# One more pair of k tiles in seven products per weight block, and two low parts of each block made by an adding DMA

## The chip, the core and the metric

One core of one Trainium2 chip runs the kernel. The metric is the device time of one execution in microseconds (us). The engines are named as in the profile: PE is TensorE (PEld its weight loads), DVE is VectorE, ACT is ScalarE, POOL is GpSimd, and SP is SyncE, which only issues transfers here. A part of the change that moves the time by less than 0.2% (2.9 us) is called no change.

## The reference, cut to what matters

A decoder layer on 256 tokens of width 2048, in float32. One projection feeds a retention branch and a windowed attention branch; both are gated, merged and projected, and a gated feed-forward network follows:

```
proj = h @ w_in                     # retention q, k, v, g; attention q, k, v; two gates
ret = retention_branch(...) ; att = sliding_window_sink_attention(...)
merged = sigmoid(gate_a) * ret + sigmoid(gate_b) * att
h = layer_norm(alpha * h + merged @ w_out)
ffn = (silu(h @ w_gate) * (h @ w_up)) @ w_down      # 5632 wide between
h = layer_norm(alpha * h + ffn)
```

Nearly all the work is in the products with the weights: h is 256 x 2048, and w_in, w_out, w_gate, w_up and w_down are read once each.

## The kernel before, in words

**Products in three passes.** Every weight block of 128 x 2048 numbers is loaded as `raw` (1 MB), rounded by ACT to `wh`, and DVE subtracts: `wl = raw - wh`. PE then adds three products, with the high part of the activations times `wh`, the high part times `wl`, and the low part times `wh`. One such product is one matmul of 128 x 128 by 128 x 512.

**Pairs in seven products.** The retention values with their gates (7 pairs of 512-column blocks, `w_ip`, called the retention pairs here) and ten of the eleven gate/up pairs (`w_gu`) are computed two column blocks at a time by `PairChunk`. Such a chunk walks over 8 pairs of k tiles. A plain pair (`s`) has 2 x 2 x 2 block products, 8 in all, so 24 matmuls. A pair taken by a scheme of seven products (`R` with 3, then `T` with 4) has 21 matmuls, but needs sums of its weight tiles: DVE makes `tsum` from `raw` in three instructions (L290 to L292), ACT rounds it to `th` (L304), DVE makes `tl` (L305); `R` takes `wh` and `wl` of three of the tiles. Sums of the activations are made once by `hsums`. `pair_seq` writes the order: `R T s R T s ...`, and the plain pairs that are left over at the end. Before, a gate/up chunk has 3 such pairs (NQ = 3) and 5 plain ones, a retention chunk 2 (NX = 2) and 6.

**Buffers.** There are 3 buffers for `wh`/`wl` (pool `spl`), shared by `R` and `s`, one for `th`/`tl` (`sp2`), one `tsum`, and 3 for `raw`. SP issues a load of `raw` as soon as the buffer's last reader is done.

**Leaving PSUM.** A chunk adds into all 8 banks: four intermediate sums and four output tiles. When the last `T` is done, `mids` copies one sum (ACT) and adds the others up (4 DVE instructions, L735 to L738); when the chunk is done, `done_gu` adds the four output tiles (L962 to L969), with a Silu of ACT between. The result `sg2` has one buffer. It is transposed by PE (L540, 8 small matmuls, two banks) in the next chunk, by a background job that `flush` starts in `mids` and `pump` advances after each step. In the retention chunks `head`, `inner` and `gate_bg` do the corresponding work.

**What sets the order.** `Stream.ahead` issues loads and casts as far ahead as the buffers allow; a scheduler then writes each engine's queue, which the engine runs in order. The gate/up pairs come in three parts, with chunks 1 to 3, 4 to 7 and 8 to 10 (chunk 0 is not a pair), and after each part four output blocks of `w_down`, whose products are plain.

Of the kernel before, what the change touches and what calls it, by code (L numbers as in the profile page):

```python
# [9 lines left out]
F32 = mybir.dt.float32  # L10
# [6 lines left out]
P = 128  # L17
# [82 lines left out]
def layer_kernel(ctx, tc, a, out):  # L100
# [58 lines left out]
    class Chunk:  # L159
        def __init__(self, src, nk, lhs, done, sizes=None, order=None, wide=False):  # L160
            self.wide = wide
            self.src, self.nk, self.lhs, self.done = src, nk, lhs, done
            sizes = sizes or [KB] * (nk // KB)
            self.blocks = []
            self.steps = []
            k = 0
            for n in sizes:
                self.blocks.append((k, n))
                for i in range(0, n, KS):
                    m = min(KS, n - i)  # L170
# [76 lines left out]
    class PairChunk:  # L247
        FORM = {"R": (("P1", "A11", 0), ("C11", "A12", 1), ("C12", "S4", 2)),
                "T": (("P5", "S1", 0), ("P7", "S3", 1), ("P6", "S2", 2), ("C21", "A22", 3))}
        def __init__(self, src, seq, lhs, lhs_s, mid, done, quiet=False):  # L250
# [34 lines left out]
        def cast(self, i):  # L285
            u, kp, b = self.steps[i]
            r = self.raw[b]
            if u == "R":
                x = sc["tp"].tile([P, 4, C], F32, name="tsum")
                nc.vector.tensor_sub(out=x[:, 0:2], in0=r[:, 0:1].broadcast_to([P, 2, C]), in1=r[:, 1:4:2])  # L290
                nc.vector.tensor_sub(out=x[:, 2], in0=r[:, 1], in1=x[:, 1])
                nc.vector.tensor_sub(out=x[:, 3], in0=r[:, 2], in1=x[:, 2])  # L292
                self.tsum = x
            if u == "T":
                h = sc["sp2"].tile([P, KS, C], F32R, name="th")
                l = sc["sp2"].tile([P, KS, C], F32R, name="tl")
# [42 lines left out]
    class Stream:  # L339
# [323 lines left out]
    sl = {}  # L663

    def head(j):
        v = gp.tile([P, 2, C], F32, name="v")
        gg = gp.tile([P, C], F32, name="gg")
        gb = gp.tile([P, C], F32, name="gb")
        nc.sync.dma_start(out=gg, in_=bcast_cols(a["gn_g"], j * C, C))
        nc.sync.dma_start(out=gb, in_=bcast_cols(a["gn_b"], j * C, C))  # L670
        y = gp.tile([P, 2, C], F32, name="y")
        sl[j] = (y, v, gg, gb)

    def done_rv(ch, t, j):
        if t == 0:
            head(j)
        y, v, gg, gb = sl[j]
        nc.scalar.copy(out=v[:, t], in_=ch.acc[t])
        if t:
            jobs["y", j] = Job(inner(j, v, y, gg, gb), [jobs["sc", j // 2]])  # L680

    def inner(j, v, y, gg, gb):
        for t in range(2):
            ps = bank("mx", [P, C])
            nc.tensor.matmul(ps, lhsT=st_all[:, j, t * P:(t + 1) * P], rhs=v[:, 0], start=True, stop=t == 0)  # L685
            if t:
                nc.tensor.matmul(ps, lhsT=st_all[:, j, 256:384], rhs=v[:, 1], start=False, stop=True)
# [53 lines left out]
    def done_va(ch, j):  # L741
# [215 lines left out]
    def done_gu(ch, f):  # L957
# [89 lines left out]
    sc["sh"] = hp.tile([P, 4, NQ, P], F32R, name="sh")  # L1047
    sc["sl"] = hp.tile([P, 4, NQ, P], F32R, name="sl")
# [104 lines left out]
```

## Time and profile before

| | |
|---|---|
| median of 3 runs | 1440.97 us (1440.94 to 1441.03) |
| the profiled execution | 1440.99 us, span 1439.2 us, so 1.8 us lie around the span |
| PE busy | 1432.2 us of the span |
| DVE busy | 1047.2 us |
| ACT busy | 673.9 us |
| POOL busy | 0.9 us |
| matmul instructions in the program | 6338 before, 6287 after |

Read it by what ends last: the share of an engine over the whole span is an average over stages with different limits, and a stage is bound by the engine on which the others wait in that stage.

### The profile page before, as it was taken

The page shows a single profiled execution, that of the slowest core. Times are in us where ns is not written, and L with a number is a line of the kernel's source. Part 1 is how long each engine was busy: PE and PEld are TensorE (multiplying, and loading weights), DVE is VectorE, ACT ScalarE, POOL GpSimd, SP SyncE. Part 2 cuts the span into 40 slices and gives each one's busy share as a digit, 9 for nine tenths or more (in the row PEclk, how much of TensorE's full clock was granted, in tenths as well). Part 3 has the DMA queues.
Part 4 walks back from the last instruction along what each step waited for, and adds up shares of the span by engine and source line. Part 5 has one row for each costly group of instructions (what it writes and reads, how often), then busy time and mean ns, then how long its engine had stood idle before and what let it go on. Part 6 is the DMA issues. An engine that isn't in the chain of part 4 may idle for free.

```text
span 1439.2 us, 16027 instructions
## 1 busy us (share of the span) xinstructions
PE 1432.2 (100%) x6536; PEld 1174.7 (82%) x6536; DVE 1047.2 (73%) x1127; ACT 673.9 (47%) x637; POOL 0.9 (0%) x6
## 2 busy tenths in 40 slices
PE   9999999999999999999999999999999999999998
PEld 7878888878878878788888888888888888888886
DVE  6764555487879879766688996567898755799756
ACT  5465444344545445444355454344555434454432
POOL 0000000000000000000000000000000000000000
PEclk9999999999999999999999999999999999999999
DMA  8643433455555655577445645555655555555562
GB/s 325 226 152 117 147 117 118 146 178 209 198 204 179 216 189 200 182 282 262 161 144 205 228 181 193 188 196 191 227 180 208 194 178 204 205 198 207 195 223 83
DMA packets 40233, 274.73 MB, mean 191 GB/s; under 512 B 4704, under 2 KB 4832, under 8 KB 8160
## 3 DMA queue, kind: packets, MB, share of 16 engines
q1 hardware_dynamic: 39440, 272.79, 53.3%
q8 instruction: 51, 0.84, 0.2%
q10 hardware_dynamic: 720, 0.92, 0.2%
q14 instruction: 22, 0.18, 0.0%
HBM read 271.60 MB, written 2.10 MB: 190 GB/s over the span
## 4 chain that ended last, share of the span: by engine, by line
PE 98%; DVE 1%; DMA 0%; ACT 0%; SPq 0%; issue 0%
PE bank L324 16%; PE bank L326 16%; PE bank L325 16%; PE acc L235 9%; PE acc L233 9%; PE acc L234 9%; PE bank L234 6%; PE bank L235 6%; PE bank L233 6%; PE tr L540 2%; PE mx L589 1%; PE mx L618 1%; PE bank L540 1%; DMA xraw<-in_xw 0%; PE bank L685 0%; PE mx L656 0%
## 5 line engine op out<-in xcount | busy, mean ns | idle before, releaser
L218 DVE TENSOR_TENSOR wl<-raw,wh 128x2048 fp32r<-128x2048 f32 x108 | 247.1, 2290 | 171.8 <-ACT wh L217 171.5
L304 ACT CAST wh<-raw 128x2048 fp32r<-128x2048 f32 (+1 forms) x136 | 241.2, 1773 | 229.2 <-PE bank L326 161.6
L217 ACT CAST wh<-raw 128x2048 fp32r<-128x2048 f32 x108 | 206.2, 1910 | 301.7 <-PE acc L235 108.5
L305 DVE TENSOR_TENSOR wl<-raw,wh 128x2048 fp32r<-128x2048 f32 (+1 forms) x136 | 287.0, 2115 | 61.7 <-ACT wh L304 61.2
L324 PE MATMUL bank<-wh,hh 128*128 128x512 f32 x460 | 179.6, 391 | 0.0
L326 PE MATMUL bank<-wh,hl 128*128 128x512 f32 x460 | 179.1, 389 | 0.0
L325 PE MATMUL bank<-wl,hh 128*128 128x512 f32 x460 | 179.0, 389 | 0.0
L324 PE MATMUL bank<-wh,xh 128*128 128x512 f32 x364 | 144.5, 397 | 0.0
L326 PE MATMUL bank<-wh,xl 128*128 128x512 f32 x364 | 141.8, 389 | 0.0
L325 PE MATMUL bank<-wl,xh 128*128 128x512 f32 x364 | 141.7, 389 | 0.0
L233 PE MATMUL acc<-wh,xh 128*128 128x512 f32 x352 | 141.0, 402 | 0.0
L235 PE MATMUL acc<-wh,xl 128*128 128x512 f32 x352 | 138.7, 394 | 0.0
L234 PE MATMUL acc<-wl,xh 128*128 128x512 f32 x352 | 137.9, 392 | 0.5 <-DVE wl L218 0.5
L233 PE MATMUL bank<-wh,ph 128*128 128x512 f32 x352 | 137.2, 390 | 0.0
L235 PE MATMUL bank<-wh,pl 128*128 128x512 f32 x352 | 137.0, 389 | 0.0
L234 PE MATMUL bank<-wl,ph 128*128 128x512 f32 x352 | 136.9, 389 | 0.0
L305 DVE TENSOR_TENSOR tl<-tsum,th 128x2048 fp32r<-128x2048 f32 x44 | 100.8, 2290 | 21.4 <-ACT th L304 21.1
L304 ACT CAST th<-tsum 128x2048 fp32r<-128x2048 f32 x44 | 84.2, 1914 | 63.1 <-DVE tsum L292 42.9
L326 PEld LDWEIGHTS bank<-wh,hl 128*128 128x128 f32 x460 | 86.4, 188 | 18.0
L324 PEld LDWEIGHTS bank<-wh,hh 128*128 128x128 f32 x460 | 86.4, 188 | 17.8
L325 PEld LDWEIGHTS bank<-wl,hh 128*128 128x128 f32 x460 | 86.4, 188 | 17.7
L324 PEld LDWEIGHTS bank<-wh,xh 128*128 128x128 f32 x364 | 68.3, 188 | 15.8 <-issue 1.4
(250 smaller groups left out, 2100.2 us busy)
## 6 DMA issues: line engine op xcount, KB each, us to landing
raw<-in_w_gu SPq DMA_DIRECT2D x88, 1024.0 KB, 4.9
raw<-in_w_ip SPq DMA_DIRECT2D x56, 1024.0 KB, 4.9
raw<-in_w_down SPq DMA_DIRECT2D x44, 1024.0 KB, 4.9
raw<-in_w_in SPq DMA_DIRECT2D x40, 1024.0 KB, 4.9
raw<-in_w_out SPq DMA_DIRECT2D x16, 1024.0 KB, 5.2
xraw<-in_xw SPq DMA_DIRECT2D x7, 768.0 KB, 6.7
hres<-in_x SPq DMA_DIRECT2D x1, 2048.0 KB, 7.5
out_h<-hres SPq DMA_DIRECT2D x5, 256.0 KB, 2.4
```

What stands on the lines that cost most here:

```text
L217: nc.scalar.copy(out=h[:, 0:m], in_=r)
L218: nc.vector.tensor_sub(out=l[:, 0:m], in0=r, in1=h[:, 0:m].bitcast(F32))
L233: nc.tensor.matmul(self.acc[t], lhsT=xh, rhs=wh[:, j], start=st, stop=False)
L234: nc.tensor.matmul(self.acc[t], lhsT=xh, rhs=wl[:, j], start=False, stop=False)
L235: nc.tensor.matmul(self.acc[t], lhsT=xl, rhs=wh[:, j], start=False, stop=sp)
L304: nc.scalar.copy(out=h_, in_=r)
L305: nc.vector.tensor_sub(out=l_, in0=r, in1=h_.bitcast(F32))
L324: nc.tensor.matmul(self.acc[p], lhsT=xh, rhs=wh[:, j], start=st, stop=False)
L325: nc.tensor.matmul(self.acc[p], lhsT=xh, rhs=wl[:, j], start=False, stop=False)
L326: nc.tensor.matmul(self.acc[p], lhsT=xl, rhs=wh[:, j], start=False, stop=sp)
L540: m = nc.tensor.transpose(ps[:, i], s, ident)
L589: nc.tensor.matmul(sps[u][:, i], lhsT=qT[u * HD:(u + 1) * HD, h // 2], rhs=kT[u * HD:(u + 1) * HD, g, 0:W], start=True, stop=True)
```

## The change

NQ goes from 3 to 4 and NX from 2 to 3: each gate/up chunk has 4 pairs in seven products and 4 plain ones, `R T s` four times over; each retention chunk has 3 and 5. In each chunk two of the plain pairs are `far`: gate/up the second and the fourth, and the retention chunks likewise two. Of a far pair DVE makes no `wl`. ACT writes `-wh` into the buffer of `wl`, and a DMA issued by POOL reads the weight block from memory a second time and adds it in place. Its load and its casts are moved ahead of the `R` and `T` of the pair of tiles before it (`corder`). The retention values `v` move into the buffers `sg`, a `drain()` is added at the end of each part, and the activation sums of the feed-forward part get a pool of their own.

```
@@ -28,8 +28,8 @@
 NWARM = 3
 TD = 14
 CP = 1
-NQ = 3
-NX = 2
+NQ = 4
+NX = 3
 PG = 4
 NGEN = 3
 PC = 2
@@ -171,6 +171,7 @@
                     self.steps.append((k + i, m, len(self.blocks) - 1, i))
                 k += n
             ns = len(self.steps)
+            self.corder = range(ns)
             self.order = order(ns) if order else [(i, (0, 1)) for i in range(ns)]
             self.raw = {}
             self.hl = {}
@@ -247,7 +248,7 @@
     class PairChunk:
         FORM = {"R": (("P1", "A11", 0), ("C11", "A12", 1), ("C12", "S4", 2)),
                 "T": (("P5", "S1", 0), ("P7", "S3", 1), ("P6", "S2", 2), ("C21", "A22", 3))}
-        def __init__(self, src, seq, lhs, lhs_s, mid, done, quiet=False):
+        def __init__(self, src, seq, lhs, lhs_s, mid, done, quiet=False, far=()):
             self.quiet = quiet
             self.src, self.blocks, self.lhs, self.lhs_s, self.mid, self.done = src, seq, lhs, lhs_s, mid, done
             self.steps = []
@@ -302,7 +310,11 @@
                 if u == "R":
                     r, h_, l_ = r[:, 1:4], h[:, 0:3], l[:, 0:3]
             nc.scalar.copy(out=h_, in_=r)
-            nc.vector.tensor_sub(out=l_, in0=r, in1=h_.bitcast(F32))
+            if i in self.far:
+                nc.scalar.activation(out=l_, in_=h_.bitcast(F32), func=AF.Copy, scale=-1.0)
+                nc.gpsimd.dma_start(out=l_, in_=self.src[kp], accum_op=ALU.add)
+            else:
+                nc.vector.tensor_sub(out=l_, in0=r, in1=h_.bitcast(F32))
             self.hl[i] = (h, l)
 
         def mm(self, i, ts):
@@ -346,9 +358,13 @@
             self.precast = {}
 
         def add(self, ch):
-            nb = len(self.blocks)
-            self.blocks += [(ch, b) for b in range(len(ch.blocks))]
-            self.casts += [(ch, i, nb + st[2]) for i, st in enumerate(ch.steps)]
+            at = {}
+            for i in ch.corder:
+                b = ch.steps[i][2]
+                if b not in at:
+                    at[b] = len(self.blocks)
+                    self.blocks.append((ch, b))
+                self.casts.append((ch, i, at[b]))
             self.steps += [(ch, i, ts) for i, ts in ch.order]
 
         def ahead(self):
@@ -663,7 +679,7 @@
     sl = {}
 
     def head(j):
-        v = gp.tile([P, 2, C], F32, name="v")
+        v = [gp.tile([P, C], F32, name="sg", bufs=4) for _ in range(2)]
         gg = gp.tile([P, C], F32, name="gg")
         gb = gp.tile([P, C], F32, name="gb")
         nc.sync.dma_start(out=gg, in_=bcast_cols(a["gn_g"], j * C, C))
@@ -800,7 +816,7 @@
     for i in range(7):
         j = (i + 1) // 2
         stream.add(PairChunk([a["w_ip"][i, kp] for kp in range(KT // 2)], pair_seq(NX), lhs_x, lhs_xs, mids,
-                             lambda ch, j=j, f=done_va if i % 2 else done_rb: f(ch, j), quiet=True))
+                             lambda ch, j=j, f=done_va if i % 2 else done_rb: f(ch, j), quiet=True, far=(NX + 1, NX + 3)))
     mark_p = len(stream.steps)
     mark_b = mark_p + 3
 
@@ -969,6 +985,7 @@
         nc.vector.tensor_mul(out=sg[:, 1], in0=sg[:, 1], in1=x5)
         ev["u"] = [(sg, t, *pTs[f]) for t in range(2)]
         if f + 1 in (4, 8, 11):
+            drain()
             flush()
 
     parts = ((0, 4), (4, 8), (8, 11))
@@ -983,7 +1000,7 @@
                 mark_u = len(stream.steps)
             else:
                 stream.add(PairChunk([a["w_gu"][f - 1, kp] for kp in range(KT // 2)], seq, lhs_h, lhs_s, mid_gu,
-                                     lambda ch, f=f: done_gu(ch, f)))
+                                     lambda ch, f=f: done_gu(ch, f), far=(NQ + 1, NQ + 3)))
         if part == 2:
             mark_e = len(stream.steps)
         nk = (f1 - f0) * 4
@@ -1056,6 +1071,9 @@
     gsc.close()
     msc.close()
 
+    hq = fsc.enter_context(tc.tile_pool(name="hq", bufs=1))
+    sc["sh"] = hq.tile([P, 4, NQ, P], F32R, name="sh")
+    sc["sl"] = hq.tile([P, 4, NQ, P], F32R, name="sl")
     ppc = ctx.enter_context(ExitStack())
     sc["pp"] = ppc.enter_context(tc.tile_pool(name="pp", bufs=4, side=RIGHT))
     sc["tp"] = ppc.enter_context(tc.tile_pool(name="tp", bufs=1, side=RIGHT))
```

How this moves instructions shows on three queues. Line numbers of the changed kernel are larger: L298 to L300 are the sums, L312 the casts, L314 the negation, L315 the adding DMA, L317 the low parts. First DVE, in the middle of the third gate/up chunk, before:

```order
L305 TENSOR_TENSOR wl_6176<-raw_6031,wh_6175 128x1536
L305 TENSOR_TENSOR wl_6214<-raw_6104,wh_6213 128x2048 [waits DMAHW3_49,Activation_49]
L305 TENSOR_TENSOR tl_6208<-tsum_6171,th_6207 128x2048 [waits Activation_49]
L290 TENSOR_TENSOR tsum_6244<-raw_6134 128x1024 [waits DMAHW4_49,DVE_49]
L291 TENSOR_TENSOR tsum_6244<-raw_6134,tsum_6244 128x512 [waits DVE_49]
L292 TENSOR_TENSOR tsum_6244<-raw_6134,tsum_6244 128x512 [waits DVE_49]
L305 TENSOR_TENSOR wl_6249<-raw_6134,wh_6248 128x1536 [waits Activation_49]
L305 TENSOR_TENSOR wl_6280<-raw_6211,wh_6279 128x2048 [waits DMAHW5_49,Activation_49]
L305 TENSOR_TENSOR tl_6274<-tsum_6244,th_6273 128x2048 [waits Activation_49]
```

and now, at the same place:

```order
L317 TENSOR_TENSOR wl_6283<-raw_6202,wh_6282 128x1536 [waits Activation_49]
L299 TENSOR_TENSOR tsum_6278<-raw_6202,tsum_6278 128x512 [waits DVE_49]
L300 TENSOR_TENSOR tsum_6278<-raw_6202,tsum_6278 128x512 [waits DVE_49]
L317 TENSOR_TENSOR tl_6303<-tsum_6278,th_6302 128x2048 [waits Activation_49]
L317 TENSOR_TENSOR wl_6338<-raw_6208,wh_6337 128x1536 [waits DMAHW4_49,Activation_49]
L298 TENSOR_TENSOR tsum_6333<-raw_6208 128x1024 [waits DVE_49]
L317 TENSOR_TENSOR wl_6369<-raw_6264,wh_6368 128x2048 [waits DMAHW5_49,Activation_49]
L299 TENSOR_TENSOR tsum_6333<-raw_6208,tsum_6333 128x512 [waits DVE_49]
L300 TENSOR_TENSOR tsum_6333<-raw_6208,tsum_6333 128x512 [waits DVE_49]
L317 TENSOR_TENSOR tl_6363<-tsum_6333,th_6362 128x2048 [waits Activation_49]
```

Before, the low parts of `R` and of a plain pair stand between the last sum and `tl`; now `tl` stands right behind the sum from which ACT must first make `th`. So it is for three of the four sums in six of the ten gate/up chunks and for one sum in another; for one of three in six retention chunks.

Second ACT, at the hand-over from the second to the third gate/up chunk, before (the two Silu are ACTIVATE of `sg2`):

```order
L304 CAST wh_6096<-raw_5986 128x1536 [waits DMAHW0_49]
L304 CAST wh_6130<-raw_6016 128x2048 [waits DMAHW1_49,PE_49,Activation_49]
L963 ACTIVATE sg2_6160<-sg2_6160 128x512 [waits DVE_49]
L304 CAST wh_6175<-raw_6031 128x1536 [waits DMAHW2_49,PE_49,Activation_49]
L966 ACTIVATE sg2_6160<-sg2_6160 128x512 [waits DVE_49]
L304 CAST wh_6213<-raw_6104 128x2048 [waits DMAHW3_49,PE_49,Activation_49]
```

and now:

```order
L312 CAST th_6198<-tsum_6160 128x2048 [waits DVE_49,PE_49,Activation_49]
L312 CAST wh_6259<-raw_6134 128x2048 [waits DMAHW2_49,PE_49]
L417 CAST ph_5945<-bank_6245 128x4x128 [waits PE_49]
L417 CAST ph_5945<-bank_6250 128x4x128 [waits PE_49]
L314 ACTIVATE wl_6260<-wh_6259 128x2048 [waits DMASW1_49,Activation_49]
L979 ACTIVATE sg2_6234<-sg2_6234 128x512 [waits DVE_49]
L982 ACTIVATE sg2_6234<-sg2_6234 128x512 [waits DVE_49]
```

The eviction of the transposed tiles and the negation for the next chunk's first far pair now stand ahead of the two Silu.

Third PE, at the same hand-over. Before, the last plain pair is followed by the next chunk's `R` (`bank` numbers are new tiles in the 8 banks):

```order
L325 MATMUL bank_5925<-wl_6028,hh_4762 128x512
L326 MATMUL bank_5925<-wh_6027,hl_4763 128x512
L324 MATMUL bank_6179<-wh_6096,hh_4762 128x512 [waits DVE_49,Activation_49]
L325 MATMUL bank_6179<-wl_6097,hh_4762 128x512 [waits DVE_49]
L326 MATMUL bank_6179<-wh_6096,hl_4763 128x512
L324 MATMUL bank_6183<-wh_6096,hh_4762 128x512
L325 MATMUL bank_6183<-wl_6097,hh_4762 128x512
L326 MATMUL bank_6183<-wh_6096,hl_4763 128x512
L324 MATMUL bank_6187<-wh_6096,sh_4764 128x512 [waits PE_49]
L325 MATMUL bank_6187<-wl_6097,sh_4764 128x512
```

and now:

```order
L338 MATMUL bank_6007<-wh_6094,hl_4825 128x512
L556 MATMUL bank_6245<-cst_80,sg2_5944 128x128 [waits Activation_49]
L556 MATMUL bank_6245<-cst_80,sg2_5944 128x128 x3
L556 MATMUL bank_6250<-cst_80,sg2_5944 128x128 [waits DVE_49]
L556 MATMUL bank_6250<-cst_80,sg2_5944 128x128 x3
L336 MATMUL bank_6266<-wh_6164,hh_4824 128x512 [waits DVE_49]
L337 MATMUL bank_6266<-wl_6165,hh_4824 128x512
L338 MATMUL bank_6266<-wh_6164,hl_4825 128x512
L336 MATMUL bank_6270<-wh_6164,hh_4824 128x512 [waits DVE_49]
L337 MATMUL bank_6270<-wl_6165,hh_4824 128x512
L338 MATMUL bank_6270<-wh_6164,hl_4825 128x512
L336 MATMUL bank_6274<-wh_6164,sh_5469 128x512 [waits DVE_49]
```

The transposes of the first chunk's result now stand at this hand-over, where before they stood two plain pairs (48 matmuls) ahead of it, and the first three products of `R` each wait for DVE to empty a bank. At the first hand-over of each of the three parts there are no transposes.

## Rows read from the trace of the kernel before

**Rows 1.** The page: busy time of the engines, and the chain by engine.

```profile
PE 1432.2 (100%) x6536; PEld 1174.7 (82%) x6536; DVE 1047.2 (73%) x1127; ACT 673.9 (47%) x637; POOL 0.9 (0%) x6
...
PE 98%; DVE 1%; DMA 0%; ACT 0%; SPq 0%; issue 0%
```

**Rows 2.** Windows: two gate/up chunks; two retention pairs. Columns in the first row.

```profile
core 0: us, PE busy (x) PEld busy (x) DVE busy (x) ACT busy (x) POOL busy (x), PEclk, DMA share, GB/s
1001.00:1042.50 41.50, 41.50 (x185) 34.36 (x184) 36.70 (x30) 21.01 (x15) 0.00 (x0) 1.00 0.57 203
1042.50:1084.70 42.20, 42.20 (x192) 35.02 (x191) 37.91 (x32) 21.75 (x17) 0.00 (x0) 1.00 0.56 199
385.67:473.56 87.89, 87.89 (x388) 71.79 (x387) 74.39 (x72) 44.05 (x34) 0.00 (x0) 1.00 0.55 196
```

**Rows 3.** Timeline of PE, 27 matmuls apart; the last `T` of that next chunk.

```profile
984.69 0.39 PE L324 MATMUL bank<-wh,hh 128*128 128x512 f32 x1
...
990.81 0.39 PE L324 MATMUL bank<-wh,hh 128*128 128x512 f32 x1
...
1043.85 0.39 PE L324 MATMUL bank<-th,sh 128*128 128x512 f32 x1
```

**Rows 4.** The chain in order of time: transposes of one gate/up result.

```profile
1052.18 0.87 PE bank L540 x8
```

**Rows 5.** Timeline of DVE in gate/up chunks: start, duration, idle before and releaser.

```profile
994.32 2.29 DVE L305 TENSOR_TENSOR wl<-raw,wh 128x2048 fp32r<-128x2048 f32 x1 [0.71 <-ACT wh L304]
...
1001.80 1.23 DVE L290 TENSOR_TENSOR tsum<-raw 128x1024 f32<-128x1024 f32 x1 [2.15 <-DMA raw<-in_w_gu]
...
1011.89 2.29 DVE L305 TENSOR_TENSOR tl<-tsum,th 128x2048 fp32r<-128x2048 f32 x1 [0.74 <-ACT th L304]
1014.10 1.75 DVE L305 TENSOR_TENSOR wl<-raw,wh 128x1536 fp32r<-128x1536 f32 x1
...
1021.15 0.68 DVE L964 TENSOR_TENSOR w<-w,bank 128x512 f32<-128x512 f32 x1
1021.75 0.68 DVE L965 TENSOR_TENSOR sg<-vx,bank 128x512 f32<-128x512 f32 x1
...
1030.64 1.22 DVE L290 TENSOR_TENSOR tsum<-raw 128x1024 f32<-128x1024 f32 x1
...
1033.37 1.76 DVE L305 TENSOR_TENSOR wl<-raw,wh 128x1536 fp32r<-128x1536 f32 x1
...
1038.56 2.29 DVE L305 TENSOR_TENSOR tl<-tsum,th 128x2048 fp32r<-128x2048 f32 x1 [0.47 <-ACT th L304]
...
1055.41 1.28 DVE L402 TENSOR_TENSOR pl<-bank,ph 128x512 fp32r<-128x512 f32 x2
```

**Rows 6.** Timeline of DVE in a retention pair, one sum and its `tl`.

```profile
441.07 0.68 DVE L292 TENSOR_TENSOR tsum<-raw,tsum 128x512 f32<-128x512 f32 x1
443.73 2.29 DVE L305 TENSOR_TENSOR tl<-tsum,th 128x2048 fp32r<-128x2048 f32 x1 [1.98 <-ACT th L304]
```

**Rows 7.** Groups by line and form: count, busy us, mean ns, idle before.

```profile
L305 DVE TENSOR_TENSOR wl<-raw,wh 128x2048 fp32r<-128x2048 f32 x92 | 210.0, 2288 | 54.3 <-ACT wh L304 54.1
...
L304 ACT CAST wh<-raw 128x2048 fp32r<-128x2048 f32 x92 | 176.0, 1913 | 156.8 <-PE bank L326 111.6 <-issue 36.9 <-PE bank L235 7.9
...
L304 ACT CAST wh<-raw 128x1536 fp32r<-128x1536 f32 x44 | 65.2, 1482 | 72.4 <-PE bank L326 50.0 <-issue 11.9 <-DVE hres L881 7.0
```

**Rows 8.** DMA issues: count, size, median us from issue to landing.

```profile
raw<-in_w_gu SPq DMA_DIRECT2D x88, 1024.0 KB, 4.9
raw<-in_w_ip SPq DMA_DIRECT2D x56, 1024.0 KB, 4.9
```

**Rows 9.** Waits of SP's queue: us in total, times, longest.

```profile
SPq L282 <- DVE wl L305: 569.7, 119, 9.2
```

More of the change, by code (lines that the diff above doesn't have):

```diff
@@ L30 @@
 CP = 1
-NQ = 3
-NX = 2
+NQ = 4
+NX = 3
 PG = 4
@@ L173, in __init__ @@
             ns = len(self.steps)
+            self.corder = range(ns)
             self.order = order(ns) if order else [(i, (0, 1)) for i in range(ns)]
@@ L249, in layer_kernel, with __init__ @@
                 "T": (("P5", "S1", 0), ("P7", "S3", 1), ("P6", "S2", 2), ("C21", "A22", 3))}
-        def __init__(self, src, seq, lhs, lhs_s, mid, done, quiet=False):
+        def __init__(self, src, seq, lhs, lhs_s, mid, done, quiet=False, far=()):
             self.quiet = quiet
@@ L266, in __init__ @@
             self.last_s = max([i for i, st in enumerate(self.steps) if st[0] == "T"], default=-1)
+            self.far = {i for i, st in enumerate(self.steps) if st[0] == "s" and st[1] in far}
+            self.corder = []
+            for i, (u, kp, b) in enumerate(self.steps):
+                at = len(self.corder)
+                if i in self.far:
+                    at -= 2 if self.steps[i - 1][0] == "T" else 1
+                self.corder.insert(at, i)
         def parts(self, u, kp):
@@ L304, in cast @@
             nc.scalar.copy(out=h_, in_=r)
-            nc.vector.tensor_sub(out=l_, in0=r, in1=h_.bitcast(F32))
+            if i in self.far:
+                nc.scalar.activation(out=l_, in_=h_.bitcast(F32), func=AF.Copy, scale=-1.0)
+                nc.gpsimd.dma_start(out=l_, in_=self.src[kp], accum_op=ALU.add)
+            else:
+                nc.vector.tensor_sub(out=l_, in0=r, in1=h_.bitcast(F32))
             self.hl[i] = (h, l)
@@ L348, in add @@
         def add(self, ch):
-            nb = len(self.blocks)
-            self.blocks += [(ch, b) for b in range(len(ch.blocks))]
-            self.casts += [(ch, i, nb + st[2]) for i, st in enumerate(ch.steps)]
+            at = {}
+            for i in ch.corder:
+                b = ch.steps[i][2]
+                if b not in at:
+                    at[b] = len(self.blocks)
+                    self.blocks.append((ch, b))
+                self.casts.append((ch, i, at[b]))
             self.steps += [(ch, i, ts) for i, ts in ch.order]
@@ L665, in head @@
     def head(j):
-        v = gp.tile([P, 2, C], F32, name="v")
+        v = [gp.tile([P, C], F32, name="sg", bufs=4) for _ in range(2)]
         gg = gp.tile([P, C], F32, name="gg")
@@ L677, in done_rv @@
         y, v, gg, gb = sl[j]
-        nc.scalar.copy(out=v[:, t], in_=ch.acc[t])
+        nc.scalar.copy(out=v[t], in_=ch.acc[t])
         if t:
@@ L684, in inner @@
             ps = bank("mx", [P, C])
-            nc.tensor.matmul(ps, lhsT=st_all[:, j, t * P:(t + 1) * P], rhs=v[:, 0], start=True, stop=t == 0)
+            nc.tensor.matmul(ps, lhsT=st_all[:, j, t * P:(t + 1) * P], rhs=v[0], start=True, stop=t == 0)
             if t:
-                nc.tensor.matmul(ps, lhsT=st_all[:, j, 256:384], rhs=v[:, 1], start=False, stop=True)
+                nc.tensor.matmul(ps, lhsT=st_all[:, j, 256:384], rhs=v[1], start=False, stop=True)
             yield 1
@@ L745, in done_va @@
         y, v, gg, gb = sl[j]
-        nc.vector.tensor_add(out=v[:, 0], in0=s1, in1=acc["C11"])
+        nc.vector.tensor_add(out=v[0], in0=s1, in1=acc["C11"])
         nc.vector.tensor_add(out=w, in0=w, in1=acc["C12"])
-        nc.vector.tensor_add(out=v[:, 1], in0=vx, in1=acc["C21"])
+        nc.vector.tensor_add(out=v[1], in0=vx, in1=acc["C21"])
         nc.vector.tensor_add(out=x5, in0=x5, in1=acc["C22"])
@@ L802, in layer_kernel @@
         stream.add(PairChunk([a["w_ip"][i, kp] for kp in range(KT // 2)], pair_seq(NX), lhs_x, lhs_xs, mids,
-                             lambda ch, j=j, f=done_va if i % 2 else done_rb: f(ch, j), quiet=True))
+                             lambda ch, j=j, f=done_va if i % 2 else done_rb: f(ch, j), quiet=True, far=(NX + 1, NX + 3)))
     mark_p = len(stream.steps)
@@ L971, in done_gu @@
         if f + 1 in (4, 8, 11):
+            drain()
             flush()
@@ L985, in layer_kernel @@
                 stream.add(PairChunk([a["w_gu"][f - 1, kp] for kp in range(KT // 2)], seq, lhs_h, lhs_s, mid_gu,
-                                     lambda ch, f=f: done_gu(ch, f)))
+                                     lambda ch, f=f: done_gu(ch, f), far=(NQ + 1, NQ + 3)))
         if part == 2:
```

9 lines of the change are left out of this document (5 added, 4 removed).

## The prediction

> **What bounds the kernel now.** I read the page first: PE is busy for all of the span but 7 us, and the chain that ended last is PE for 98% [rows 1]. So each matmul that goes is worth its pitch, as long as the operands keep coming. A row of PE gives 390 ns for a matmul, but that is its latency. The pitch is read from the timeline: 27 matmuls lie between 984.69 and 990.81 us, so 0.2267 us each [rows 3]. Then I asked how much room the engines that feed PE have where the change acts. The windows show it: in a gate/up chunk of 42.2 us DVE works 37.9 us, in two retention pairs 74.4 of 87.9 us [rows 2]. DVE is the engine that can become the bound; ACT works half of the time and POOL not at all [rows 1, 2]. DVE is also not far ahead: the last `tl` of one chunk ends at 1038.56 + 2.29 = 1040.85 us [rows 5], and PE starts on it at 1043.85 us [rows 3]. The lead is 3.0 us.
>
> **The change part by part.**
>
> *Matmuls.* Each of the 17 chunks turns one pair of 24 matmuls into one of 21. That is 51 matmuls; 51 x 0.2267 = **-11.6 us**. A gate/up chunk then takes PE 180 x 0.2267 = 40.8 us, and 41.7 us where the transposes (0.87 us [rows 4]) lie in it; before, 183 x 0.2267 + 0.87 = 42.4 us.
>
> *DVE's work.* Steps from start to start [rows 5]: three sums 2.73 us (1030.64 to 1033.37), a `tl` or a whole `wl` 2.21 (1011.89 to 1014.10), the `wl` of an `R` by the same overlap of 0.08 us 1.75 - 0.08 = 1.67, an addition from PSUM 0.60 (1021.15 to 1021.75), two evicted low parts 1.2. Before: 3 x (2.73 + 1.67 + 2.21) + 5 x 2.21 + 10 x 0.60 + 1.2 = 38.1 us, which the window confirms with 37.9. Now: 4 x 6.61 + 2 x 2.21 + 7.2 = 38.1 us. The fourth pair adds 6.6 us; with one plain pair gone and two far ones made by DMA, three `wl` go, which gives the same back. In a retention chunk it is 2 x 6.61 + 6 x 2.21 before and 3 x 6.61 + 3 x 2.21 now, again the same. So the work costs nothing, but it must fit into a shorter chunk.
>
> *DVE's waits in gate/up.* This is the term on which the sign rests. In the new order `tl` stands right behind the third sum in three of four cases, so DVE stands still while ACT makes `th`. The trace has that wait in a retention pair: 1.98 us [rows 6]. Three of them are 5.9 us a chunk. Elsewhere before, other low parts stood between, and 0.47 to 0.74 us of it were left [rows 5]. Next, the sum of the fourth pair needs the `raw` buffer that the third pair's sum and low part release. From such a release to the next sum the trace shows 5.2 us (996.61, the end of the `wl` that starts at 994.32, to 1001.80, waiting on the DMA [rows 5]; SP waits for releases of this kind 119 times [rows 9]). Between the two sums lie 1.98 + 2.21 = 4.2 us, so 1.0 us is a wait. DVE's queue then takes 38.1 + 5.9 + 1.0 = 45.0 us from one last `tl` to the next, against 40.8 or 41.7 us of PE. The lead hides 3.0 us of it, once in each part, because the plain `w_down` blocks after a part give the lead back (DVE needs 2.29 us for each 24 x 0.2267 = 5.44 us of matmuls there). The first hand-over of a part costs 45.0 - 40.8 - 3.0 = 1.2 us, the second 45.0 - 41.7 = 3.3; the third one in the middle part has only one such wait (45.0 - 2 x 1.98 = 41.0) and costs nothing. Over three parts: 3 x 4.5 = **+13.5 us**. Bounds: 0, if the lead is larger or ACT earlier, and 18 us, if each of the seven hand-overs also loses the 0.6 us by which the two Silu stand later behind the negation.
>
> *DVE's waits in retention.* One such wait in six of seven chunks, 11.9 us of DVE. The one wait of this kind in the trace cost PE nothing [rows 1, 6], and DVE's 74.4 + 4 us fit into 87.9 - 1.4 us [rows 2]. But the evictions come in bunches, and fewer steps are left behind `mids` to spread them. Between 0 and 11.9 us I take a value near the row that cost nothing: **+2 us**.
>
> *Adding DMAs.* The trace has none; POOL issues no DMA before. A far buffer comes free when the plain pair before it is done, and is used after `R T s R T`, 66 matmuls or 15.0 us later. ACT's cast, the cast of an `R` and the negation take 1.91 + 1.48 + 1.91 = 5.3 us [rows 7], so 9.7 us are left. Below, an add lands like a load, after 4.9 us [rows 8]. Above: the DMA share of 0.57 over 41.5 us [rows 2] is 2.96 us of all engines for each of 8 loads; an add that reads its target too takes them twice, 4.9 + 2.96 = 7.9 us, and behind one load 10.8 us. I take 7.9, nearer to the row of a lone load, so **0 us**; at 10.8 it would be 1.1 us for each of 34 adds, +37 us. The engines' share rises to (8 x 2.96 + 2 x 5.9) / 41.7 = 0.85, so there is room in sum. The Trainium skill, Collectives: The Full Stack, The bandwidth ceiling, says that adding in the DMA path is half as fast as copying only because of its second source read; by that an add takes the engines twice, an estimate of 7.9 us, which no row here can show.
>
> *At nothing.* ACT gains 34 negations (65 us) and 17 more casts of an `R` (25 us); it goes from 674 to some 764 us of 1439 [rows 1], under PE. Uncovered, it is the Silu's 0.6 us above. One more pass of `hsums` on either side of the middle lies in a chunk of plain blocks, where DVE works 2.29 of 5.44 us; uncovered, five instructions of at most 0.68 us each, 3.4 us. `v` in `sg` and the new pool add no instruction.
>
> Sum: -11.6 + 13.5 + 2 + 0 = +3.9 us on the profiled execution's 1440.99 us (span 1439.2 plus 1.8 around it), which is 0.02 us above the median: **1445 us**, 0.3% slower.
>
> **The rivals.**
>
> *A (forecast): DVE's queue gives the saving back.* 1445 us, own range 1438 to 1453.
>
> *B: faster.* DVE's waits vanish under PE. For it: DVE idles for 42.4 - 38.1 = 4.3 us in each chunk now, PE does not notice, and the new PE order puts up to 8 matmuls of the next plain pair between those of `T`, so that `tl` is needed up to 8 x 0.2267 = 1.8 us later. It decides if a lead of over 45.0 - 40.8 + 3.3 = 7.5 us a part is there, where the rows show 3.0. Then 1440.99 - 11.6 = 1429.4, up to 1437 with half of the 13.5 us left.
>
> *C: the adds land late.* From 9.7 us after the negation on, PE waits for the far `wl`. Against it is the lone load's 4.9 us; for it, that loads are under way for over half of the time (share 0.57 [rows 2]). With 10.8 us: 1440.99 - 11.6 + 37 = 1466 us, since DVE catches up while PE waits and its 13.5 us go under. The Trainium skill, DMA: Bandwidth & Descriptors, Issuing engines are not separate DMA queues, speaks for this one: transfers from POOL run on the same 16 engines as SP's and interleave with them, so POOL's own queue gives an add no bandwidth of its own.
>
> *D: nothing changes,* the waits being 11 us by chance; it is the inside of A.
>
> **How the numbers follow.** A 0.47, B 0.30, C 0.20, 0.03 for the rest. Under A the time is below 1438.1 in 0.02, within 0.2% of 1441 (1438.1 to 1443.9) in 0.18, above in 0.27. Faster: 0.30 + 0.02 = 0.32. Same: 0.18. Slower: 0.27 + 0.20 + 0.03 = 0.50. The predicted time is A's, 1445. The range must reach into B and C: from 1430, which leaves out the lower end of B (0.08), to 1472, which leaves out adds later than 11 us (0.12).
>
> **What would show it.** Right: matmuls at the same pitch and 51 fewer; idle time of PE, a few us in each of the chunks 2, 3, 5, 6, 9 and 10, put down to DVE (`tl`, or a bank); DVE with waits of about 2 us on `th`, and on `raw` at the fourth pair. B would show PE without such gaps; C would show PE waiting for a DMA queue at the second and fourth plain pair, and adds of over 9.7 us. The prediction is wrong if DVE gets further ahead than 3 us in the plain blocks, or if the adds slow the loads so much that every sum waits for `raw`.

## The result and the profile after

1478.58 us (median of 4 runs, 1476.15 to 1481.02) against 1440.96 us: ratio 1.0261, 95% interval 1.0243 to 1.0279. The changed kernel is 37.6 us slower, outside the forecast range. The profiled execution took 1476.15 us, its span is 1474.3 us: 35.1 us more than before.

The page of the changed kernel: busy time, the chain, the DMA queues (packets, MB, share of 16 engines) and the median landing times (compare [rows 1, 8]).

```profile
PE 1437.0 (97%) x6485; PEld 1168.1 (79%) x6485; DVE 1042.3 (71%) x1173; ACT 759.1 (51%) x690; POOL 30.4 (2%) x40
...
q1 hardware_dynamic: 39440, 272.79, 51.5%
q0 software_dynamic: 4896, 35.65, 12.9%
...
PE 70%; DMA 9%; DVE 9%; ACT 6%; issue 6%; SPq 0%; ACTq 0%; DVEq 0%; POOLq 0%
...
raw<-in_w_gu SPq DMA_DIRECT2D x88, 1024.0 KB, 4.9
raw<-in_w_ip SPq DMA_DIRECT2D x56, 1024.0 KB, 5.1
...
wl<-in_w_gu POOLq DMA_DIRECT2D x20, 1024.0 KB, 8.6
...
wl<-in_w_ip POOLq DMA_DIRECT2D x14, 1024.0 KB, 10.3
```

The chain was 98% PE; now 30% of it is DMA, DVE, ACT and issue. The 34 adds (q0) take 12.9% of the span on all engines, 5.59 us each; for q1, which moved as much as 260 loads of this size in 51.5%, the same sum gives 2.92 us a load. The forecast's estimate of a doubled time is right; the median landing of 8.6 and 10.3 us is above its 7.9.

The waits of the changed kernel (engine, line, releaser: us in total, times, longest):

```profile
PE bank L337 <- DMA wl<-in_w_gu: 15.6, 7, 4.0
PE bank L337 <- DVE wl L317: 8.7, 4, 4.4
PE bank L336 <- DVE pl L418: 3.0, 4, 1.7
PE bank L337 <- DMA wl<-in_w_ip: 1.9, 2, 1.1
...
DVE tl L317 <- ACT th L312: 66.5, 33, 4.0
...
DVE tsum L298 <- DMA raw<-in_w_ip: 17.0, 5, 6.2
```

PE waits for adds in gate and up. DVE's waits on `th` are there as forecast, 33 of them with 66.5 us in all, more than in the kernel before:

```profile
DVE tl L305 <- ACT th L304: 21.1, 25, 2.4
```

Sums in retention wait 17.0 us for `raw`; before, it was 1.9 us.

Windows of the same kernel: retention up to the first gate/up pair, that pair to the end, and 4 us behind four of PE's waits (of 3.59, 3.96, 4.44 and 1.41 us). Third from the right is the granted clock.

```profile
324.20:776.60 452.40, 441.54 (x1940) 359.02 (x1939) 344.80 (x359) 245.72 (x185) 12.25 (x14) 0.99 0.72 230
776.60:1474.30 697.70, 674.12 (x2951) 548.84 (x2949) 500.78 (x435) 350.82 (x239) 17.34 (x20) 0.99 0.68 217
...
905.40:909.40 4.00, 3.98 (x11) 3.16 (x12) 0.95 (x2) 0.00 (x0) 0.00 (x0) 0.60 0.98 401
...
1389.20:1393.20 4.00, 3.98 (x9) 3.14 (x10) 0.61 (x1) 0.00 (x0) 0.00 (x0) 0.50 0.94 381
396.20:400.20 4.00, 3.99 (x9) 3.14 (x10) 4.00 (x5) 0.00 (x0) 0.00 (x0) 0.50 0.76 256
1126.50:1130.50 4.00, 4.00 (x18) 3.31 (x19) 4.00 (x5) 1.92 (x1) 0.00 (x0) 1.00 0.46 141
```

Behind the longer waits the clock falls to its lower level for a while (0.50 is 1.2 of 2.4 GHz), and 9 to 12 matmuls pass in 4 us instead of 17 or 18. In some of these windows the clock is not yet back at the end. Windows of 8 us behind the five longest waits (396.2, 857.2, 905.4, 1080.7 and 1389.2 us) show 0.70, 0.79, 0.79, 0.81 and 0.68, so the lower level costs about 8 x (0.30 + 0.21 + 0.21 + 0.19 + 0.32) = 9.8 us, 7.4 of them in gate and up.

From PE's timeline I cut every run at two places, the first `S4` product of retention and that of gate and up. Us of each stage; the ideal is before less 21 and 30 matmuls of 0.2267 us:

| | retention to gate/up | gate/up to the end |
|---|---|---|
| before | 441.6 | 673.3 |
| ideal | 436.8 | 666.5 |
| changed kernel | 452.4 | 697.7 |
| e_small | 440.5 | 673.3 |
| e_load | 446.7 | 673.3 |
| e_one1 / e_one | 439.8 / 449.4 | 679.7 / 693.9 |
| e_nofar | 437.4 | 672.9 |
| pin_dve | 437.4 | 667.7 |
| pin_small | 437.8 | 671.1 |
| pin_adds | 454.3 | 671.1 |
| pin_ret1 / pin_ret2 | 442.3 / 445.3 | 671.2 / 671.3 |

The stages are those of the profiled executions; with full adds the time varies by 5 us and more from run to run (pin_adds 1445.25 to 1451.59, its profiled one with 1449.8 of span at the upper end), with plain loads in e_load by 6, with short transfers or none by some 2 at most.

Against the ideal the changed kernel lost 31 us in gate and up (forecast 13.5) and 15.6 in retention (forecast 2).

### The profile page after: what moved, and what is told of

Same layout as the page of the kernel before. It is cut to its first block, busy times and chain, and to the rows that moved or that the text cites. A ratio compares the mean times of both kernels' runs of the same rounds, so it can differ in the third digit from the quotient of the medians.

```text
span 1474.3 us, 16144 instructions
## 1 busy us (share of the span) xinstructions
PE 1437.0 (97%) x6485; PEld 1168.1 (79%) x6485; DVE 1042.3 (71%) x1173; ACT 759.1 (51%) x690; POOL 30.4 (2%) x40
## 3 DMA queue, kind: packets, MB, share of 16 engines
q1 hardware_dynamic: 39440, 272.79, 51.5%
q0 software_dynamic: 4896, 35.65, 12.9%
## 4 chain that ended last, share of the span: by engine, by line
PE 70%; DMA 9%; DVE 9%; ACT 6%; issue 6%; SPq 0%; ACTq 0%; DVEq 0%; POOLq 0%
PE bank L337 8%; PE bank L338 8%; PE acc L234 8%; PE acc L236 8%; PE bank L336 8%; PE acc L235 8%; PE bank L236 5%; PE bank L235 5%; PE bank L234 5%; DMA wl<-in_w_gu 5%; DVE wl L317 3%; DMA raw<-in_w_ip 3%; ACT wh L312 2%; PE tr L556 2%; PE mx L605 1%
## 5 line engine op out<-in xcount | busy, mean ns | idle before, releaser
L312 ACT CAST wh<-raw 128x2048 fp32r<-128x2048 f32 (+1 forms) x136 | 232.8, 1717 | 182.9 <-PE bank L338 153.3
L317 DVE TENSOR_TENSOR wl<-raw,wh 128x1536 fp32r<-128x1536 f32 (+1 forms) x102 | 200.3, 1967 | 58.1 <-ACT wh L312 57.7
L317 DVE TENSOR_TENSOR tl<-tsum,th 128x2048 fp32r<-128x2048 f32 x61 | 139.7, 2290 | 67.1 <-ACT th L312 66.5
L337 PE MATMUL bank<-wl,hh 128*128 128x512 f32 x400 | 159.6, 399 | 15.6 <-DMA wl<-in_w_gu 15.6
L312 ACT CAST th<-tsum 128x2048 fp32r<-128x2048 f32 x61 | 116.4, 1908 | 102.2 <-DVE tsum L300 94.6
L336 PE MATMUL bank<-wh,hh 128*128 128x512 f32 x400 | 159.1, 398 | 1.3 <-DVE pl L418 1.3
L338 PE MATMUL bank<-wh,hl 128*128 128x512 f32 x400 | 157.7, 396 | 0.0
L337 PE MATMUL bank<-wl,xh 128*128 128x512 f32 x322 | 127.5, 396 | 10.7 <-DVE wl L317 8.7
L336 PE MATMUL bank<-wh,xh 128*128 128x512 f32 x322 | 127.5, 398 | 0.0
L338 PE MATMUL bank<-wh,xl 128*128 128x512 f32 x322 | 126.6, 393 | 0.0
L298 DVE TENSOR_TENSOR tsum<-raw 128x1024 f32<-128x1024 f32 x61 | 74.5, 1221 | 20.0 <-DMA raw<-in_w_ip 17.0
## 6 DMA issues: line engine op xcount, KB each, us to landing
wl<-in_w_ip POOLq DMA_DIRECT2D x14, 1024.0 KB, 10.3
```

What stands on the lines that cost most here:

```text
L336: nc.tensor.matmul(self.acc[p], lhsT=xh, rhs=wh[:, j], start=st, stop=False)
L337: nc.tensor.matmul(self.acc[p], lhsT=xh, rhs=wl[:, j], start=False, stop=False)
L338: nc.tensor.matmul(self.acc[p], lhsT=xl, rhs=wh[:, j], start=False, stop=sp)
```

## The experiments

The theory (L): the adds land later than PE asks. The rival (O): the waits in DVE's order, larger than forecast.

**e_small: short adds, the same order.**

```
-nc.gpsimd.dma_start(out=l_, in_=self.src[kp], accum_op=ALU.add)
+nc.gpsimd.dma_start(out=l_[:, 0, 0:C // 4], in_=self.src[kp][:, 0, 0:C // 4], accum_op=ALU.add)
```

> The changed kernel with every adding DMA cut to the first 128 columns of one block (64 KB in place of 1024 KB); the far low parts are then mostly -h, so the output is not the reference's. Every instruction of PE, DVE and ACT stands where it stood. Theory L (the adds land late and slow the raw loads, and PE waits for them): of the 46.7 us of new waits only those behind DVE's order stay, so 1440.97 - 11.6 + 5 to 14 = 1434 to 1443 us; no wait of PE on the POOL queue, no wait of DVE on raw over 1 us, and the granted clock stays at full after 390, 857, 905, 1080 and 1389 us. Rival O (DVE's waits on th, as forecast, only larger than forecast): the adds' size does not matter, 1470 to 1479 us.

1438.39 us, ratio 0.9983 (0.9974 to 0.9992). O fell, as the whole cause: 40 us hang on the adds' size. DVE's waits on `th` are unchanged (66.5 us), and no wait of PE is on a POOL transfer:

```profile
PE bank L337 <- DVE wl L317: 2.6, 1, 2.6
PE bank L336 <- DVE x L754: 1.8, 3, 0.6
PE bank L336 <- DVE pl L418: 1.6, 1, 1.6
```

One thing that L expected did not come: DVE still waits for `raw` in retention, 9.0 us in all and up to 4.4 us at once. More on this below.

**e_gu and e_ret: each stage alone** (`NX = 2` and no `far` in retention; `NQ = 3` and no `far` in gate and up).

> The change in the gate and up pairs alone: four k pairs and two adding DMAs there, the retention and gate chunks with two k pairs and no adding DMA, as before. By the starts of the chunks in the trace the gate/up stage lost 31 us and won 30 x 0.2267 = 6.8 us, so if the two stages do not touch each other 1441 + 24 = 1465 us (1462 to 1468), for theory L as for rival O. If the late adds of the first stage cost something in the second one it is less than 1462.

> The change in the retention and gate pairs alone: three k pairs and two adding DMAs there, gate and up with three k pairs and no adding DMA, as before. By the starts of the chunks that stage lost 15.5 us and won 21 x 0.2267 = 4.8 us: 1441 + 10.7 = 1452 us (1449 to 1455). With the gate/up run it should add up to the whole change, +37.6 us.

1467.29 us (ratio 1.0178, 1.0142 to 1.0214) and 1452.87 us (1.0085, 1.0070 to 1.0100). 26.3 + 11.9 = 38.2 us against 37.6: the stages add up.

**e_nofar: the additional k pairs without adding DMAs** (both `far=` left out).

> One more k pair in seven products in both stages, but no adding DMA: DVE makes all low parts, in the order of the program. DVE has 2 x 2.21 us more in each chunk, 42.5 us against 40.8 to 41.7 us of PE, and some waits on th. Theory L: it costs what DVE lacks, about 2 to 3.5 us in each of 10 gate/up chunks less the lead of 3 us a part, and up to 2 in a retention chunk: 1441 - 11.6 + 15 to 35 = 1444 to 1465 us, less than the changed kernel. Rival O: DVE is the bound in both, and this one has more work in it: 1478 us or more.

1436.29 us, ratio 0.9968 (0.9956 to 0.9979): faster than before, and some 8 us below the lower end of what I had expected. DVE has more work (1115 us) but waits only 24.3 us on `th`, since the low parts that it makes itself stand in those gaps.

**e_one1 and e_one: one add a chunk, the earlier or the later one** (`far=(NX + 1,)` and `(NQ + 1,)`; then `(NX + 3,)` and `(NQ + 3,)`).

> Of the two adding DMAs of a chunk only the one for the second plain pair is left (17 of 34); the low part of the fourth plain pair is made by DVE in its old place. In the run with short adds the first kind was issued 13.1 us before PE asked for it (853.29 to 866.40 us) in gate and up, 9.4 us in retention. Theory L (an add costs only where it lands after PE asks): at 8 to 9 us it is in time, so 1432 to 1439 us, with no wait of PE on the POOL queue in gate and up. Rival K (what costs is the second transfer as such, through the loads that share the engines): half of the adds, half of the 40 us, 1452 to 1462 us.

> The other way round: only the add for the fourth plain pair (gate and up) and the third plain pair (retention) is left, the one that in the run with short adds was issued 7.7 us before PE asked for it (877.88 to 885.61 us). Theory L: a lone add lands after 7.8 us or more, so nearly each of the 10 gate/up chunks waits 0.5 to 2 us and the clock falls behind the longer waits: 1440 to 1455 us, clearly above the run with the other add. Rival K: the same as that one, 1452 to 1462 us.

1447.47 us (1.0048, 1.0033 to 1.0063) and 1468.09 us (1.0188, 1.0164 to 1.0213). Both sizes were off, and so was K: the same number of adds costs 20 us more in one place than in the other. The place is not the only difference, though: the low part that DVE makes again stands at another place too, and DVE waits 31.4 us for `th` in e_one1 and 43.7 in e_one. The landing times of e_one1, then of e_one:

```profile
wl<-in_w_gu POOLq DMA_DIRECT2D x10, 1024.0 KB, 8.4
```

```profile
wl<-in_w_gu POOLq DMA_DIRECT2D x10, 1024.0 KB, 11.8
```

A late add not only has less time, it takes longer. The early one was not free: in e_one1 PE still waited 3.2 us for adds.

**e_load: a plain load in place of the add** (`accum_op` left out).

> The changed kernel with a plain load of the same 1024 KB from the same queue in place of each adding DMA (nothing is added, so the far low parts are the weights themselves and the output is not the reference's); every instruction stands where it stood. A load takes the 16 engines for about 2.96 us, an add by the trace 5.6. Theory L: it lands in 5 to 7 us, before the 7.7 us are over, so 1436 to 1443 us. A rival, that any 1 MB transfer from POOL's queue is late and holds up SP's loads, gives 1460 to 1479 us.

1446.46 us (1.0037, 1.0025 to 1.0049). The transfers landed in 5.5 us, and gate and up take 673.3 us, the time of the short adds. So there the price hangs on what the add takes beyond a load, and not on POOL's queue. Retention loses 6.2 us (446.7 - 440.5), which I had not expected: there a plain load does part of the harm.

**e_pool: POOL makes the far low parts.**

```
-nc.scalar.activation(out=l_, in_=h_.bitcast(F32), func=AF.Copy, scale=-1.0)
-nc.gpsimd.dma_start(out=l_, in_=self.src[kp], accum_op=ALU.add)
+nc.gpsimd.tensor_sub(out=l_, in0=r, in1=h_.bitcast(F32))
```

> The far low parts are made by one subtraction on POOL in place of negation and adding DMA: 34 subtractions of 128 x 2048 on an engine that stands idle, no second transfer, ACT 65 us less. No row of POOL tells how long it takes. Theory L has a time only by its condition: up to about 7.7 us and with DVE undisturbed it hides, 1430 to 1440 us; if it takes longer, or DVE's rows get longer while POOL works, PE waits at the same places as in the changed kernel, 1450 us or more.

1536.57 us (1.0666, 1.0646 to 1.0687). Groups by form of this run: POOL's subtraction, and DVE's first sum:

```profile
L314 POOL TENSOR_TENSOR wl<-raw,wh 128x2048 fp32r<-128x2048 f32 x34 | 173.5, 5103 | 1270.7 <-ACT wh L312 1235.2 <-DVE x L777 35.6
```

```profile
L298 DVE TENSOR_TENSOR tsum<-raw 128x1024 f32<-128x1024 f32 x61 | 100.2, 1643 | 15.7 <-DMA raw<-in_w_ip 13.8 <-DMA raw<-in_w_gu 1.2
```

5.1 us is below the 7.7 that the expectation allowed, but DVE's first sum takes 1643 ns instead of 1221: DVE is disturbed. The mean mixes two kinds: by DVE's and POOL's timelines the ten of the 61 sums that overlap a subtraction of POOL take 3.8 us on the mean, the other 51 take 1.22. The Trainium skill, SBUF — State Buffer, Who interferes with whom, says that a DVE instruction with two SBUF inputs contends with a POOL instruction that reads SBUF; these rows agree. How the 98 us by which this run is slower than e_small divide stays open.

**The pin: DVE's waits filled.** On DVE the low part of `R` may stand anywhere after its cast; pinned, it stands between the last sum and `tl`, in the time in which ACT makes `th`.

```
-nc.vector.tensor_sub(out=l_, in0=r, in1=h_.bitcast(F32))
+m = nc.vector.tensor_sub(out=l_, in0=r, in1=h_.bitcast(F32))
+if u == "R":
+    tc.keep_in_program_order(m)
```

pin_dve is e_nofar with it, pin_adds the changed kernel, pin_small e_small, pin_mix as pin_dve with `pair_seq(3 if f in (2, 6, 9) else NQ)`.

> The run without adding DMAs, and the low part of each R pinned to its place in the program, so that on DVE it stands between the last sum and tl and fills the time in which ACT makes th. DVE has 42.5 us of work in a gate/up chunk, as in the run without adding DMAs, and no wait on th. Theory L (what is left of the loss once the adds are gone is DVE's waits on th): of the 6.9 us by which the run without adding DMAs misses 1440.97 - 11.6, 1.7 us a chunk over PE less the lead of 3 us a part stays, so 1430 to 1435 us. Rival O2 (what is left is DVE's work, not its waits): 1436 us again.

> The changed kernel, adding DMAs and all, with the low part of each R pinned in the same way. Theory L: the adds are as late as before, so most of the 40 us stays, 1465 to 1478 us, and PE still waits on the POOL queue in gate and up. Rival O (DVE's order is the cause after all, and the late adds only show where DVE makes PE late): 1445 us or less.

> The same with the adds cut to 64 KB (the far low parts are mostly -h, so the output is not the reference's); DVE has 38.1 us of work in a gate/up chunk and no waits of 2 us on th. Theory L: DVE then fits under PE's 40.8 us, so nearly the whole saving shows: 1429.5 to 1433 us. If the 9 us that the run with short adds misses come from the hand-overs (evictions, Silu, banks) it stays at 1436 to 1439 us.

> As the first of these, but the chunks 2, 6 and 9 of gate and up with three k pairs in seven products, so that DVE's 38.1 us there against 42.4 us of PE give back the lead that the others use. 9 matmuls more on PE, 2.0 us. If DVE's work of 42.5 us is what is left, this run is level with the first or up to 2 us faster; if nothing is left there, it is 2.0 us slower.

pin_dve: **1431.12 us, ratio 0.9932 (0.9919 to 0.9946)**, the fastest of all, 1.7 us above before less 11.6. O2 fell: more work on DVE than in the changed kernel, and PE does not wait for it. Its page, and DVE's timeline from a last sum to the next first one (the low part of `R` and one `wl`, then `tl` without a wait; compare [rows 6]):

```profile
PE 1420.6 (99%) x6485; PEld 1163.8 (81%) x6485; DVE 1119.1 (78%) x1207; ACT 702.3 (49%) x656; POOL 0.9 (0%) x6
...
PE 93%; DVE 5%; issue 1%; ACT 1%; DMA 0%; SPq 0%; ACTq 0%; DVEq 0%
```

```profile
1029.77 0.69 DVE L300 TENSOR_TENSOR tsum<-raw,tsum 128x512 f32<-128x512 f32 x1
1030.38 3.95 DVE L317 TENSOR_TENSOR wl<-raw,wh 128x1536 fp32r<-128x1536 f32 x2
1034.26 2.28 DVE L317 TENSOR_TENSOR tl<-tsum,th 128x2048 fp32r<-128x2048 f32 x1
1036.57 1.23 DVE L298 TENSOR_TENSOR tsum<-raw 128x1024 f32<-128x1024 f32 x1
```

pin_small 1435.18 (0.9960, 0.9947 to 0.9974), between its two cases. pin_mix 1432.49 (0.9941, 0.9928 to 0.9953): 1.4 us slower than pin_dve for 2.0 us of matmuls, so DVE's work in pin_dve costs PE no more than 0.6 us at these places.

pin_adds: 1447.6 us (1.0049, 1.0035 to 1.0063). **Here theory L fell in its simple form.** I had put 1465 to 1478; one pin on DVE took 31 us away, and in gate and up the adds now cost nothing (671.1 us, as in pin_small). The two timelines show why. The changed kernel, the far step at the end of a chunk, on ACT, POOL and PE:

```profile
886.41 1.91 ACT L312 CAST th<-tsum 128x2048 fp32r<-128x2048 f32 x1 [5.58 <-DVE tsum L300]
888.22 3.51 ACT L312 CAST wh<-raw 128x2048 fp32r<-128x2048 f32 x2
891.63 1.91 ACT L314 ACTIVATE wl<-wh 128x2048 fp32r<-128x2048 f32 x1
...
893.90 0.86 POOL L315 DMA_DIRECT2D wl<-in_w_gu  x1 [23.61 <-ACT wl L314]
...
901.45 0.39 PE L336 MATMUL bank<-wh,hh 128*128 128x512 f32 x1
905.42 0.50 PE L337 MATMUL bank<-wl,hh 128*128 128x512 f32 x1 [3.59 <-DMA wl<-in_w_gu]
```

The same step in pin_adds:

```profile
883.97 1.92 ACT L312 CAST wh<-raw 128x2048 fp32r<-128x2048 f32 x1 [3.47 <-PE bank L340]
885.91 1.92 ACT L314 ACTIVATE wl<-wh 128x2048 fp32r<-128x2048 f32 x1
...
888.19 0.86 POOL L315 DMA_DIRECT2D wl<-in_w_gu  x1 [19.83 <-ACT wl L314]
...
898.95 0.39 PE L339 MATMUL bank<-wl,hh 128*128 128x512 f32 x1
```

In pin_adds ACT's far cast waits for nothing but its buffer (PE). In the changed kernel it stands on ACT behind `th`, and `th` waits 5.58 us for DVE's late sum; the cast starts at 888.22 us, 1.8 us after the last matmul on its buffer (886.04 + 0.39). Then the cast of an `R` stands between it and the negation (the second of the two in that row); in pin_adds that cast comes later, which saves 1.5 us more. So the pin, set on DVE, has moved ACT's order too, and its 31 us are the worth of both. The add of the changed kernel is issued 7.8 us before PE asks (901.45 + 0.23 - 893.90), not 10.8 (898.95 - 888.19). And it meets other traffic. DMA issues in the windows 893 to 906 us of the changed kernel and 887.5 to 898 us of pin_adds:

```profile
raw<-in_w_down SPq DMA_DIRECT2D x3, 1024.0 KB, 6.8
wl<-in_w_gu POOLq DMA_DIRECT2D x1, 1024.0 KB, 11.5
```

```profile
wl<-in_w_gu POOLq DMA_DIRECT2D x1, 1024.0 KB, 9.2
raw<-in_w_down SPq DMA_DIRECT2D x1, 1024.0 KB, 8.0
```

11.5 us against 7.8 is the wait that PE shows; 9.2 against 10.8 is none. Two of the three loads were issued only at 901.45 and 903.65 us, when PE was about to wait already; that they are what made this add slower than 9.2 us is likely, and no run changes it alone.

The other late adds of gate and up are alike. In all seven ACT has a `th` right ahead of the far cast or, once, between it and the negation, and in six this `th` had waited 5.1 to 5.6 us for DVE's sum. PE asked 6.7 to 9.0 us after the issue, 8.2 on the mean, and the adds landed after 7.9 to 12.0 us, 10.5 on the mean.

**before_pin, pin_ret1 and pin_ret2.** before_pin is the kernel before with the pin; the other two are pin_adds with `far=(NX + 1,)` and `far=(NX + 1, NX + 4)` in retention.

> Control: the kernel before with the low part of each R pinned in the same way, nothing else. If DVE's order was hidden under PE there, as its chain of 98% PE says, the time stays within 0.2% of 1441 us, and what the run with the pin and without adding DMAs won belongs to the additional k pairs; if the pin pays by itself, 1432 to 1437 us.

> The changed kernel with the pin, and in retention and gate only the first of the two adding DMAs of a chunk; gate and up keep both. Theory M (in retention two adds some 10.8 us after each other meet the loads, and one load then takes some 10 us, so that DVE's sums wait for raw; a lone add does no harm): the 16.6 us that retention loses against the run with the pin and short adds go, 1434 to 1438 us. Rival (each add costs about its share of engine time there): half of it stays, 1441 to 1446 us.

> The same with both adding DMAs in retention and gate, but the second one for the last plain pair of a chunk in place of the last but one, so that the two stand some 5 us further apart and the second is away from the sums. Theory M: most of the loss goes, 1435 to 1442 us, and DVE waits for raw less than 19 us. Rival: two adds are two adds, 1445 to 1451 us as in the run with the pin.

before_pin: 1440.87 us (0.9999, 0.9990 to 1.0009). The pin alone wins nothing; pin_dve's gain is the k pairs' with DVE's waits out of the way. pin_ret1: 1439.87 (0.9994, 0.9985 to 1.0003). pin_ret2: 1444.14 (1.0025, 1.0016 to 1.0034). Both lie between theory M and its rival. A lone add in retention is not free (PE waits 3.7 us for three of them), two cost more, and further apart less. DVE's wait for `raw` in retention fell from 19.4 us in pin_adds to 14.9 in pin_ret2 and 4.5 in pin_ret1. How it reaches PE stands in the chain of the changed kernel:

```profile
382.23 10.40 DMA raw<-in_w_ip
...
392.72 0.09 DVE tsum L298
...
393.87 2.30 DVE wl L317
...
396.21 0.79 PE bank L337
```

A load of a size that lands in 4.9 us on the median took 10.40 beside an add issued at 382.36 us (the one before, of 371.59, had landed at 380.15, so theory M's two adds after each other are not what it met); the sum, the low part and PE follow. The same load in the chains of e_load, beside a plain load of POOL's queue, and of e_small, beside an add of 64 KB:

```profile
381.70 10.65 DMA raw<-in_w_ip
```

```profile
380.87 8.60 DMA raw<-in_w_ip
```

So this load is slow without full adds too, and the doubled time of an add alone is not its cause. With the pin it took 5.92 us beside a short add (pin_small) and 11.72 beside a full one (pin_adds). What slows it stays open. Elsewhere in retention the adds do lengthen the loads: the slowest one takes 11.4 us in the changed kernel (issued at 478.7 us) and 7.8 at that place in e_load. Of retention's 16.5 us in pin_adds (454.3 - 437.8) the waits of PE tell the larger part:

```profile
PE bank L339 <- DVE wl L317: 10.8, 4, 5.9
PE bank L339 <- DMA wl<-in_w_ip: 2.5, 2, 1.4
```

Three of the four waits on DVE (5.88, 1.63 and 1.65 us) end a chain that starts with a load of 11.72, 9.55 and 9.16 us; only 2.5 us are waits for the adds themselves.

## Why the prediction was wrong

- **Matmuls, -11.6: right.** 6536 to 6485 instructions, and 27 matmuls of the changed kernel lie between 879.01 and 885.13 us, so the pitch is 0.2267 us as before.

```profile
879.01 0.39 PE L336 MATMUL bank<-wh,hh 128*128 128x512 f32 x1
...
885.13 0.39 PE L337 MATMUL bank<-wl,hh 128*128 128x512 f32 x1
```

- **DVE's waits in gate/up, +13.5: the waits came, their price was too high.** The order and the waits of 2 us on `th` came as described. With short adds, in the changed kernel's order, the stage takes 673.3 us, 6.8 above the ideal, half of the forecast. And not all of that is the mechanism that was forecast: PE has no wait on `tl` there, but one of 1.6 us on an eviction (`pl`) and three of 0.6 us on a bank (`x`). The pin took DVE's waits on `th` from 66.5 to 23.9 us in both stages together and won 2.2 us here (673.3 - 671.1).
- **Retention, +2:** 440.5 - 436.8 = 3.7 us with short adds, inside 0 to 11.9. That it is near is partly luck: 2.6 us of it are the one wait of PE behind the load of 8.60 us, which the forecast did not have.
- **The adds, 0: the step that failed.** "So 9.7 us are left" counted ACT's work (5.3 us) from the moment when the buffer comes free. It forgot what else stands on ACT's queue: `th`, which waits for DVE's sum. The issue came later, and for the seven late adds of gate and up 6.7 to 9.0 us were left. "I take 7.9" was right in the add's engine time, but it put no load beside the add; these seven landed after 10.5 us on the mean, 2.6 later than that, while the time that was left fell from 9.7 to 8.2 on the mean; so the landing is the larger of the two errors. The price is 697.7 - 673.3 = 24.4 us in gate and up (15.6 of it waits of PE on adds, some 7.4 the clock) and 452.4 - 440.5 = 11.9 in retention, there mostly through late loads. The sum is -11.6 + 6.8 + 3.7 + 24.4 + 11.9 = +35.2 us; measured 35.1. It has to close, since its terms are differences of measured stages.
- **Rival C was the right case, and its 1466 too low.** It had every add 1.1 us late. In fact few are late, but by up to 4 us, the clock falls behind them (9.8 us with retention, in no part of my sum), and late loads stop DVE's sums in retention. Its remark that DVE's 13.5 us would go under the adds' waits had the dependence the wrong way round: in gate and up DVE's waits, handed on through ACT's queue, made the adds late, and with most of them filled no wait on an add was left there.
- **The rules cited.** What the forecast took from the Trainium skill, DMA: Bandwidth & Descriptors, Issuing engines are not separate DMA queues, agrees with the trace: loads beside POOL's transfers and adds beside loads take longer. So does Collectives: The Full Stack, The bandwidth ceiling, of the Trainium skill: an add takes the engines 1.9 times as long as a load (5.59 against 2.92 us).
- **Open:** with the pin and short adds gate and up still lose 4.6 us, with the pin and no adds 1.2. Negations on ACT, the moved casts and the short transfers differ; which of them it is, no run shows. The waits of PE on `vx` and `pl` are 3.3 us in pin_small and 0.7 in pin_dve.
